# Products of the first token pair of an output projection, placed among the steps of the last attention

## The chip, the cores and the metric

The kernel runs on one core of a Trainium2 chip. The core has a matrix engine (PE in the profile, with its weight loads as PEld), a vector engine (DVE), a scalar engine (ACT), a second vector engine (POOL) and a queue processor (SP) that here issues every DMA. Each of them takes its instructions strictly in the order in which the program lists them. The metric is the time of one execution on the device in microseconds (us); lower is better.

## The reference

One decoder layer over 2048 tokens of width 1024, with 16 learned tokens put in front. Three mixers read one normalized input projection, and their gated outputs are joined to y, 2048 channels wide. What this case is about is the last of the mixers and the output projection:

```python
o_fox = fox_attention(q, k, v, log_f, valid)        # 8 heads of 64, causal
y_fox = o_fox * silu(fg)
y = concatenate([y_fox, y_gla, y_lru]) * vmask      # 2048 channels
h = h + rms_norm(y @ w_out, post_g)                 # (L,2048) @ (2048,1024)
```

## The kernel before

All of it is one unrolled program, scheduled by a framework: the Python code traces instructions in some order, a scheduler then lists them for each engine by priority (earlier traced first) and by the moment at which it thinks their inputs and buffers are ready, and it allots the buffers. `issue_after(x)` adds that an instruction may not stand before `x` on `x`'s engine. The resulting lists are fixed when the kernel is built.

**The attention.** The head pairs p = 0..3 are worked off in four chunks of 512 queries (c = 0..3). `fox_attend(k, p, c)` has 4c + 5 steps, so the last one, (3, 3), has 17, j = 0..16. A step makes the scores of 128 keys (eight matmuls into the one pair of PSUM banks `sq`), lets ACT exponentiate them into `pt` (L1305), lets DVE and POOL add `pt` to the running sums `za` (L1313), and multiplies `pt` of an earlier step with the values (`fv`, L1325). After the last step the sums go through a matmul (L1336, `fx<-za`), and the row of sums then travels: ACT copies it (L506), a DMA writes it to DRAM (L508), another brings it back spread over partitions (L510), DVE takes reciprocals (L1342, L1343), a DMA writes these (L515), two more bring them back as `rz` (L1349), POOL multiplies (L1351) and a DMA stores the attention's output into `yD` (L1352). For all chunks but the last these steps are done inside the next chunk's attention; for the last they come at its end (`end_late`).

**What runs beside it.** `merge(mix, prep, n_main, n_fill)` advances an attention and the preparation of the next job side by side; what is left of either is drained at the end. Beside the last attention runs `out_begin`, with n_fill = `OB` = 16: it loads y for the first two token blocks (t = 0, 1), loads four of the seven weight blocks (B11, T2, B21, T3) into the place where the normalized input `xhl` lay, waits nine steps, and then makes the first five parts of the halves of y (`pair_halves`).

**The output projection.** Two blocks of 128 tokens and both halves of the 1024 columns are done by a Winograd scheme with seven products in place of eight: A11·B11, S2·T2, A12·B21, S3·T3, S1·T1, A22·T4, S4·B22. Each factor is a sum of two f16 halves, so a product is 3 x 8 matmuls of 512 columns, 24 in all, on one of two PSUM banks `pj`. A pair of blocks takes 168 matmuls, and there are eight pairs (t = 0, 2, .. 14). For each pair `pair_halves` makes, on ACT, DVE and POOL: squares of y (L459), a power-of-two scale from them (DVE cast L470, a small matmul L472, DVE L316 to L320), and then for each of the seven left factors a high half on ACT (L1475) and a low half on DVE (L1476), with the sums S1 to S4 made by POOL and DVE (L1519 to L1532). `project_out` first loads the other three weight blocks (T1, T4, B22) into twelve tiles `ts`, then runs the pairs; `product` calls `next(ahead)` after each product, so that the halves are made ahead of their use: before the change five parts of a pair's halves are traced before the pair begins. `Out.finish` normalizes, adds x and stores.

All weight and y loads are 512 KB each. The lines of this document for L1475 to L1614 are those of the kernel before; the change moves them by 12 to 24 lines (L1604 becomes L1616, L1488 becomes L1512).

Of the kernel before, what the change touches and what calls it, by code (L numbers as in the profile page):

```python
# [12 lines left out]
F16 = mybir.dt.float16  # L13
I32 = mybir.dt.int32
U8 = mybir.dt.uint8
AF = mybir.ActivationFunctionType
# [5 lines left out]
P = 128  # L22
D = 1024
KT = D // P
NM = 16
SEQ = 2048
T = NM + SEQ
CH = 512
# [46 lines left out]

OB = 16
WOUT = (95, 150)
GAP = 2  # L80
FA0 = (0, 0, 1, 3, 4, 5)
# [6 lines left out]
class Ctx:  # L88
# [8 lines left out]
BUFS = {"A0": 3, "A2": 3, "KA": 6, "KB": 6, "QA": 2, "QB": 2, "B0": 2, "B1": 2, "B2": 2, "B3": 2, "V": 6, "G": 2, "R": 1,  # L97
        "T": 3, "ZZ": 8, "WR": 6, "WT": 2, "WS": 2, "TS": 12, "WC": 1, "OO": 3, "OX": 2, "LV": 5, "AT": 2, "AC": 2, "GV": 6, "GG": 6, "GS": 6, "M": 1, "MV": 1, "YG": 2, "RS": 2, "ZS": 1, "ZA": 2, "PT": 6, "ED": 2, "KT": 1, "Z": 1, "WH": 1, "WL": 1, "XC": 4, "X": 16, "L0": 4, "L1": 4, "L2": 2, "L3": 2, "L4": 6}


def unit(k, tag, shape, dt=F32, name=None):
    wide = tag in ("AT", "QA", "QB", "KA", "KB", "WC", "OO", "OX", "T", "Z", "ZZ", "WH", "WL")
    n = 1
    for d in shape[1:]:
        n *= d
    full = k.wk.tile([P, 2 * CH if wide else CH], dt, name=name or tag, tag=tag, bufs=BUFS[tag])
    ap = full[0:shape[0], 0:n]
    if len(shape) == 3:
        ap = ap.rearrange("p (a b) -> p a b", b=shape[2])
    return ap  # L110
# [39 lines left out]
def drain(g):  # L150
    for _ in g:
        pass
# [15 lines left out]
def hybrid_kernel(tc, xT, x, w_grp, w_fa, vecs, w_a2, w_r, w_i, w_out, post_g, masks, out, yD=None):  # L168
    nc = tc.nc
    with ExitStack() as es:  # L170
# [63 lines left out]
        for i, (_, _, mix, n_main, _) in enumerate(jobs):  # L234
            if i + 1 < len(jobs):
                _, prep, _, _, n_fill = jobs[i + 1]
            else:
                prep, n_fill = out_begin(k), OB
            k.todo += jobs[i][0]
# [1123 lines left out]
BLOCKS = ("B11", "T2", "B21", "T3", "T1", "T4", "B22")  # L1363
# [75 lines left out]
def wout_load(k, nm, w):  # L1439

    with k.tc.issue_after(k.mark):
        for z in range(2):
            for j in range(2):
                mark = k.nc.sync.dma_start(out=w[2 * z + j], in_=k.wD[BLOCKS.index(nm), z, j]).ins
    k.W[nm] = w
    return mark


def out_begin(k):

    nc = k.nc
    k.mark = k.dr
    k.W = {}
    n = 4 * KT // 2 * P
    views = [[k.xhl[:, (4 * i + z) * n:(4 * i + z + 1) * n].rearrange("p (q k n) -> p q k n", q=4, n=P)
              for z in range(4)] for i in range(4)]
    k.winv = k.xhl[:, 16 * n:16 * n + 2 * CH].bitcast(F32)
    raws = pair_load(k, 0)
    for i in range(4):
        k.load = wout_load(k, BLOCKS[i], views[i])  # L1460
    for q in range(4):
        nc.gpsimd.tensor_scalar(out=k.winv[:, P * q:P * q + P], in0=k.ones, scalar1=k.winvs[q], scalar2=None,
                                op0=ALU.mult)
    for _ in range(9):
        yield
    k.pairs = pair_halves(k, 0, raws)
    for _ in range(5):
        with k.tc.issue_after(k.exp):
            next(k.pairs)
        yield  # L1470


def halves(k, x, sc, hi, lo):
# [5 lines left out]
def tile4(k, tag, name):  # L1479
    return unit(k, tag, [P, KT, P], name=name)  # L1480


def y_load(k, t):
    yv = k.yD.rearrange("(h t p) n -> h p t n", p=P, h=2)
    raws = [tile4(k, "ZZ", "y") for _ in range(2)]
    for h in range(2):
        with k.tc.issue_after(k.mark):
            k.load = k.nc.sync.dma_start(out=raws[h], in_=yv[h, :, :, P * t:P * t + P]).ins  # L1488
    return raws


def y_halves(k):
    hl = k.wp.tile([P, 2, KT, P], F16, name="whl", bufs=NWB)
    return hl[:, 0], hl[:, 1]


def pair_load(k, t):
    return y_load(k, t) + y_load(k, t + 1)


def pair_halves(k, t, raws):


    nc = k.nc
    a11, a12, a21, a22 = raws
    junk = k.wk.tile([P, KT, P], BF16, name="junk", tag="A2", bufs=BUFS["A2"])
    ss = squares(k, [(x, junk) for x in (a11, a12, a21, a22)], scale=2.0)
    yield
    sc, inv = scale_of(k, ss)
    d = k.st["pair", t] = dict(inv=inv)  # L1510

    def put(nm, x):  # L1512
        d[nm] = y_halves(k)
        halves(k, x, sc, *d[nm])

    put("A11", a11)
    yield
    s1, s2 = tile4(k, "T", "s1"), tile4(k, "T", "s2")
    nc.gpsimd.tensor_tensor(s1, a21, a22, op=ALU.add)  # L1519
    nc.vector.tensor_tensor(s2, s1, a11, op=ALU.subtract)  # L1520
    put("S2", s2)
    yield
    put("A12", a12)
    yield
    nc.gpsimd.tensor_tensor(a21, a11, a21, op=ALU.subtract)
    put("S3", a21)
    yield
    put("S1", s1)
    yield
    put("A22", a22)  # L1530
    yield
    nc.gpsimd.tensor_tensor(s2, a12, s2, op=ALU.subtract)  # L1532
    put("S4", s2)


def project_out(k):
    nc = k.nc
    NT = SEQ // P
    k.mark = k.load
    for nm in BLOCKS[4:]:  # L1540
        wout_load(k, nm, [k.wk.tile([P, 4, KT // 2, P], F16, name="ts", tag="TS", bufs=BUFS["TS"])
                           for _ in range(4)])
    pg = unit(k, "WC", [P, 2, CH], name="pg")
    k.pg = [pg[:, h, :] for h in range(2)]
    with k.tc.issue_after(k.store):
        nc.sync.dma_start(out=pg.rearrange("p h n -> p (h n)"), in_=k.ins["post_g"].to_broadcast([P, 2 * CH]))
    for t in range(0, NT, 2):
        more = pair_halves(k, t + 2, pair_load(k, t + 2)) if t + 2 < NT else iter(())
        out_pair(k, t, chain(k.pairs, more))
        k.pairs = more  # L1550


class Out:
# [38 lines left out]
def out_pair(k, t, ahead):  # L1592

    nc = k.nc
    d = k.st.pop(("pair", t))
    inv = d["inv"]

    def product(nm, w):
        ps = bank(k, "pj")
        yh, yl = d.pop(nm)  # L1600
        w = k.W[w]
        for kt in range(KT):
            for j, (a, b) in enumerate(((yh, 0), (yh, 2), (yl, 0))):
                nc.tensor.matmul(out=ps, lhsT=a[:, kt, :], rhs=w[b + kt // 4][:, :, kt % 4, :], start=kt + j == 0,  # L1604
                                 stop=(kt, j) == (KT - 1, 2))
        next(ahead, None)
        return ps

    def add(ps, x, y):
        nc.vector.scalar_tensor_tensor(out=y, in0=ps, scalar=inv, in1=x, op0=ALU.mult, op1=ALU.add)  # L1610

    oa, ob = Out(k, t), Out(k, t + 1)
    c11, c12, c21, c22 = (o.o[:, n, :] for o in (oa, ob) for n in range(2))
    nc.scalar.activation(c11, product("A11", "B11"), AF.Copy, scale=inv)  # L1614
    add(product("S2", "T2"), c11, c12)
    add(product("A12", "B21"), c11, c11)  # L1616
    oa.scaled(0)
    add(product("S3", "T3"), c12, c21)
    ps = product("S1", "T1")
    add(ps, c21, c22)  # L1620
    add(ps, c12, c12)
    ob.scaled(1)
    add(product("A22", "T4"), c21, c21)
    ob.scaled(0)
    ob.finish()
    add(product("S4", "B22"), c12, c12)
    oa.scaled(1)
    oa.finish()

# [45 lines left out]
```

## Time and profile before

| | us |
|---|---|
| median of three timed runs | 1989.29 (1987.2 to 1992.66) |
| the profiled execution, its own time | 1977.47 |
| its span, first to last instruction | 1975.8 |
| PE busy in the span | 1880.4 (95%) |
| DVE, ACT, POOL busy | 1268.3, 1012.7, 565.4 |
| projection matmuls (L1604) busy: on `xhl` and on `ts` weights | 168.6 and 125.7 |

The terms below are read from the profiled execution, which was 11.8 us faster than the median of the timed ones. The page cuts the span into 40 equal slices of 49.4 us. PE is at nine tenths or more in nearly all of them; slices 32 and 33 (about 1581 to 1680 us, the end of the attention) read 8 and 7, and the clock granted to PE reads 8 in both. The DMA engines, at four tenths or less since slice 1, read 8 and 7 in slices 33 and 34.

### The profile page before, as it was taken

How to read it: one execution, taken by the hardware profiler on the slowest of the kernel's cores; microseconds unless marked ns; L12 is line 12 of the kernel's file. 1: busy time of each engine (PE TensorE's matmuls, PEld its weight loads, DVE VectorE, ACT ScalarE, POOL GpSimd, SP SyncE). 2: the span in 40 equal slices, each digit the busy share in tenths (PEclk: the TensorE clock that was granted, in tenths of full speed). 3: DMA queues.
4: the chain of work that ended last, by engine and by line, in shares of the span. 5: the costliest groups of instructions: out<-in, count | busy, mean ns of one | idle time of the engine just before them, and what ended most of it. 6: DMA issues, size and time to landing. Idle time of an engine off the chain costs nothing. (4 is left out here: it accounts for less than half of the span.)

```text
span 1975.8 us, 39430 instructions
## 1 busy us (share of the span) xinstructions
PE 1880.4 (95%) x15988; PEld 976.2 (49%) x15988; DVE 1268.3 (64%) x2850; ACT 1012.7 (51%) x1561; POOL 565.4 (29%) x548
## 2 busy tenths in 40 slices
PE   6888999999999999999999999999999987999997
PEld 5555666666555555555434443444344422444443
DVE  6766454454787788673665368747874665667674
ACT  7755642344888887762345234523442335444441
POOL 3443133221434333320122111211221124433422
PEclk9999999999999999999999999999999988999999
DMA  6200121211211100121132113412431128723411
GB/s 225 76 8 29 43 86 29 75 55 30 82 52 45 44 22 22 43 74 44 61 101 69 30 46 118 128 45 65 118 97 44 44 59 294 234 87 122 134 43 64
DMA packets 116135, 152.69 MB, mean 77 GB/s; under 512 B 18793, under 2 KB 75817, under 8 KB 115953
## 3 DMA queue, kind: packets, MB, share of 16 engines
q1 hardware_dynamic: 115952, 150.18, 24.0%
q8 instruction: 125, 2.05, 0.4%
q14 instruction: 58, 0.47, 0.1%
HBM read 108.71 MB, written 41.33 MB: 76 GB/s over the span
## 5 line engine op out<-in xcount | busy, mean ns | idle before, releaser
L485 PE MATMUL pj<-xhl,whl 128*128 128x512 f16 (+3 forms) x3960 | 813.1, 356 | 16.1 <-ACT whl L437 7.4
L485 PEld LDWEIGHTS <-whl 128*128 128x128 f16 x3984 | 364.8, 98 | 405.1 <-issue 80.7
L1305 ACT ACTIVATE pt<-sq,consts 128x1024 f32<-128x1024 f32 (+4 forms) x176 | 163.4, 929 | 252.5 <-PE sq L1303 97.7
L1313 POOL TENSOR_TENSOR za<-za,pt 128x512 f32<-128x512 f32 (+1 forms) x80 | 99.0, 1238 | 535.4 <-ACT pt L1305 489.1
L1239 DVE CUSTOM_DVE_ANT_0 mj<-mq,CB 128x512 bf16<-128x512 f32 (+4 forms) x344 | 189.9, 579 | 56.7 <-PE mq L1231 28.5
L1604 PEld LDWEIGHTS <-whl 128*128 128x128 f16 x1344 | 130.6, 98 | 160.6 <-issue 4.4
L497 PEld LDWEIGHTS <-xhl 128*128 128x128 f16 (+1 forms) x3264 | 184.9, 97 | 31.6 <-issue 27.3
L497 PE MATMUL pj<-whl,xhl 128*128 128x128 f16 (+1 forms) x3024 | 189.6, 219 | 0.0
L1313 DVE TENSOR_TENSOR za<-za,pt 128x512 f32<-128x512 f32 (+3 forms) x208 | 121.3, 606 | 84.6 <-ACT pt L1305 81.2
L1325 PE MATMUL fv<-pt,fv 128*64 128x512 f32 (+4 forms) x688 | 171.3, 538 | 0.0
L1604 PE MATMUL pj<-xhl,whl 128*128 128x512 f16 x768 | 168.6, 380 | 0.0
L1297 PE MATMUL sq<-QA,KA 64*128 64x512 f16 (+4 forms) x1032 | 127.0, 341 | 9.5 <-ACT pt L1305 9.5
L1604 PE MATMUL pj<-ts,whl 128*128 128x512 f16 x576 | 125.7, 379 | 0.0
L563 DVE SCALAR_TENSOR_TENSOR xc<-lx,consts,xc 128x448 f32<-128x448 f32 (+1 forms) x120 | 93.4, 778 | 3.6
L1588 POOL TENSOR_TENSOR o<-o,xt 128x512 f32<-128x512 f32 x31 | 51.6, 1684 | 120.3 <-issue 91.7
L1570 ACT ACTIVATE sqo<-o 128x512 bf16<-128x512 f32 x32 | 20.1, 630 | 127.7 <-DVE o L1564 127.7
L521 ACT ACTIVATE gate<-pj,consts 128x512 f32<-128x512 f32 (+2 forms) x72 | 46.1, 641 | 72.4 <-PE pj L485 59.4
L1297 PEld LDWEIGHTS <-KA 64*128 64x128 f16 (+1 forms) x1032 | 40.3, 94 | 82.5 <-issue 59.9
L1610 DVE SCALAR_TENSOR_TENSOR o<-pj,consts,o 128x512 f32<-128x512 f32 x56 | 41.1, 745 | 61.1 <-PE pj L1604 56.9
L598 POOL TENSOR_TENSOR v<-a 128x448 f32<-128x448 f32 (+1 forms) x40 | 38.4, 961 | 129.5 <-ACT a L596 115.4
L1231 PE MATMUL mq<-KA,QA 64*128 64x512 f16 (+4 forms) x344 | 60.8, 342 | 10.6 <-DVE consts L1239 9.0
L522 DVE SCALAR_TENSOR_TENSOR gate<-gate,pj 128x512 f32<-128x512 f32 (+2 forms) x72 | 45.1, 627 | 39.4 <-ACT gate L521 38.1
(263 smaller groups left out, 2786.4 us busy)
## 6 DMA issues: line engine op xcount, KB each, us to landing
wr<-in_w_out_dram SPq DMA_DIRECT2D x64, 256.0 KB
y<-yD SPq DMA_DIRECT2D x32, 512.0 KB
raw<-in_w_grp_dram SPq DMA_DIRECT2D x28, 512.0 KB
wD<-ws SPq DMA_DIRECT2D x56, 256.0 KB
CB<-c32D SPq DMA_DIRECT2D x32, 256.0 KB
rawf<-in_w_grp_dram SPq DMA_DIRECT2D x16, 512.0 KB
xhl<-wD SPq DMA_DIRECT2D x16, 512.0 KB
xt<-in_x_dram SPq DMA_DIRECT2D x16, 512.0 KB
```

Of the source, the lines that this page charges most:

```text
L485: nc.tensor.matmul(out=ps, lhsT=a[:, kt, 0:m], rhs=b[:, kt, u0:u0 + n], start=i == 0, stop=i == 23)
L497: nc.tensor.matmul(out=ps, lhsT=a[:, kt, u0:u0 + m], rhs=b[:, kt, :], start=i == 0, stop=i == 23)
L521: k.act = nc.scalar.activation(out, ps, AF.Tanh, scale=hinv).ins
L563: nc.vector.scalar_tensor_tensor(out=xc, in0=lx[:, j:j + n], scalar=cw(j), in1=xc, op0=ALU.mult, op1=ALU.add)
L1231: nc.tensor.matmul(out=ps[h][:, 0:n], lhsT=qh[hs, P * i:P * i + P], rhs=d.hi[pc][hs, 0:n], start=True, stop=pc < c)
L1239: nc.vector.tensor_tensor_reduce(out=junk[:, h, 0:n], in0=ps[h][:, 0:n], in1=d.cb[pc][:, h, 0:n], scale=1.0, scalar=-3e38, op0=ALU.add, op ...
L1297: nc.tensor.matmul(out=sp[0:m, h, off:], lhsT=a[j // 4][hs, kk], rhs=b[hs, off:], start=i == 0, stop=i == 3 and d < 0)
L1305: k.exp = nc.scalar.activation(pt[0:m, :, off:], sp[0:m, :, off:], AF.Exp, scale=K.esc[0:m]).ins
L1313: add = eng.tensor_tensor(out=za[h][0:m, off:], in0=za[h][0:m, off:], in1=pt[0:m, h, off:], op=ALU.add).ins
L1325: nc.tensor.matmul(out=pv[hs, off1:], lhsT=V1[0:m1, j1 % 4, hs], rhs=pt1[0:m1, h, off1:], start=j1 == 0, stop=j1 == nj - 1)
L1588: eng.tensor_tensor(out=o, in0=o, in1=xt[:, h, :], op=ALU.add)
L1604: nc.tensor.matmul(out=ps, lhsT=a[:, kt, :], rhs=w[b + kt // 4][:, :, kt % 4, :], start=kt + j == 0, stop=(kt, j) == (KT - 1, 2))
```

## The change

`out_begin` starts on the halves of y of the first pair at once: one idle step in place of nine, then eight steps that finish all seven factors. It then loads `post_g`, and goes on with the first pair's products themselves, by a new generator `out_next`. `product` yields after k-steps 1, 3 and 5, so that a third of a product's matmuls is one step. `OB` goes from 16 to 18: all that is past the 18th step is drained after the attention's own end. The loads of T1, T4 and B22 are traced when the tenth part of the products is reached. For the first pair `next(ahead)` is called only after three of the seven products, and the y of the second pair is loaded when the first of these calls comes; from then on two fewer parts of a pair's halves are made before the pair begins.

```diff
-OB = 16
+OB = 18
...
-    for _ in range(9):
-        yield
+    yield
     k.pairs = pair_halves(k, 0, raws)
-    for _ in range(5):
+    for _ in range(8):
         with k.tc.issue_after(k.exp):
-            next(k.pairs)
-        yield
+            next(k.pairs, None)
+        yield
+    k.mark = k.load
+    pg = unit(k, "WC", [P, 2, CH], name="pg")
+    k.pg = [pg[:, h, :] for h in range(2)]
+    with k.tc.issue_after(k.load):
+        nc.sync.dma_start(out=pg.rearrange("p h n -> p (h n)"), in_=k.ins["post_g"].to_broadcast([P, 2 * CH]))
+    k.mark = k.load
+    yield
+    for i, _ in enumerate(out_next(k, 0)):
+        if i == 9:
+            for nm in BLOCKS[4:]:
+                k.load = wout_load(k, nm, [k.wk.tile([P, 4, KT // 2, P], F16, name="ts", tag="TS", bufs=BUFS["TS"])
+                                           for _ in range(4)])
+            k.mark = k.load
+        yield
+
+
+def out_next(k, t):
+    more = iter(())
+    if t == 0:
+
+        more = (x for f in (lambda: pair_halves(k, 2, pair_load(k, 2)),) for x in f())
+    elif t + 2 < SEQ // P:
+        more = pair_halves(k, t + 2, pair_load(k, t + 2))
+    ahead, k.pairs = chain(k.pairs, more), more
+    yield from out_pair(k, t, ahead)
...
 def project_out(k):
-    nc = k.nc
-    NT = SEQ // P
-    k.mark = k.load
-    for nm in BLOCKS[4:]:
-        wout_load(k, nm, [k.wk.tile([P, 4, KT // 2, P], F16, name="ts", tag="TS", bufs=BUFS["TS"])
-                           for _ in range(4)])
-    pg = unit(k, "WC", [P, 2, CH], name="pg")
...
-    for t in range(0, NT, 2):
-        more = pair_halves(k, t + 2, pair_load(k, t + 2)) if t + 2 < NT else iter(())
-        out_pair(k, t, chain(k.pairs, more))
-        k.pairs = more
+    for t in range(2, SEQ // P, 2):
+        drain(out_next(k, t))
...
-        next(ahead, None)
+            if kt in (1, 3, 5):
+                yield
+        if t or nm in ("S1", "A22", "S4"):
+            next(ahead, None)
         return ps
...
-    nc.scalar.activation(c11, product("A11", "B11"), AF.Copy, scale=inv)
+    nc.scalar.activation(c11, (yield from product("A11", "B11")), AF.Copy, scale=inv)
```

What the scheduler makes of it, in two places. The first is SP's queue at the end of the last attention, from the last weight loads of the attention's time on; `ts<-wD` are tiles of T1, T4, B22, `y<-yD` is y of the second pair, and the rows from `rowD<-zs` to `yD<-fo` are the last attention's travel of sums. Before:

```order
L1444 DMA ts<-wD 128x2048
L1488 DMA y<-yD 128x8x128 x2
L508 DMA rowD<-zs 1x512 x2
L1488 DMA y<-yD 128x8x128 x2
L510 DMA consts<-rowD 128x8
L1444 DMA ts<-wD 128x2048 x2
L1488 DMA y<-yD 128x8x128
L515 DMA rowD<-consts 128x8
L1444 DMA ts<-wD 128x2048 x2
L1349 DMA rz<-rowD 64x512 x2
L1578 DMA xt<-in_x_dram 128x1024 x2
L1352 DMA yD<-fo 128x512
```

Now:

```order
L1444 DMA xhl<-wD 128x2048 x4
L1474 DMA pg<-in_post_g_dram 128x1024
L508 DMA rowD<-zs 1x512 x2
L510 DMA consts<-rowD 128x8
L515 DMA rowD<-consts 128x8
L1349 DMA rz<-rowD 64x512 x2
L1352 DMA yD<-fo 128x512
L1444 DMA ts<-wD 128x2048 x12
L1512 DMA y<-yD 128x8x128 x5
L1590 DMA xt<-in_x_dram 128x1024
```

All twelve `ts` loads and the y of the second pair moved from before and among the travel of sums to behind its last DMA; before, eight of the twelve `ts` loads, the eighth in the first row shown, stood ahead of the travel.

The second is ACT, from the first step of the last attention on; `pt<-sq` is a step's exponential, `junk<-y` a square, `whl` a high half. Before:

```order
L1305 ACTIVATE pt<-sq,consts 128x1024 x10
L459 ACTIVATE junk,consts<-y 128x1024 x2
L1305 ACTIVATE pt<-sq,consts 128x1024
L459 ACTIVATE junk,consts<-y 128x1024 x2
L1305 ACTIVATE pt<-sq,consts 128x1024
L1475 ACTIVATE whl<-y,consts 128x1024
L1475 ACTIVATE whl<-s_19419,consts 128x1024
L1305 ACTIVATE pt<-sq,consts 128x1024
```

Now:

```order
L1305 ACTIVATE pt<-sq,consts 128x1024
L459 ACTIVATE junk,consts<-y 128x1024 x2
L1305 ACTIVATE pt<-sq,consts 128x1024
L459 ACTIVATE junk,consts<-y 128x1024
L1305 ACTIVATE pt<-sq,consts 128x1024
L459 ACTIVATE junk,consts<-y 128x1024
L1305 ACTIVATE pt<-sq,consts 128x1024
L1499 ACTIVATE whl<-y,consts 128x1024
L1499 ACTIVATE whl<-s_19284,consts 128x1024
L1499 ACTIVATE whl<-y,consts 128x1024
L1305 ACTIVATE pt<-sq,consts 128x1024
```

The squares moved from behind the tenth exponential to behind the first, and three high halves now stand ahead of the fifth exponential (step j = 4). On PE, 60 of the first pair's matmuls now stand ahead of the attention's closing matmul L1336 (ten behind step 4's scores, two in each of the next seven steps, then 6, 6, 6, 12 and 6), where 18 stood before; behind L1336 come 36 on `xhl` weights and 72 on `ts` weights, where there were 78 and 72.

## Rows read from the trace of the kernel before

**Rows 1.** Windows view: stretch, its length; busy (count) by engine; PEclk, DMA share, GB/s.
```profile
1624.00:1676.00 52.00, 41.09 (x229) 12.11 (x225) 30.77 (x39) 28.89 (x33) 22.86 (x12) 0.89 0.87 302
1624.50:1632.10 7.60, 7.35 (x35) 1.65 (x32) 1.99 (x3) 3.94 (x4) 1.77 (x1) 0.77 1.16 314
...
1711.00:1950.00 239.00, 239.00 (x1130) 108.62 (x1129) 157.45 (x205) 99.02 (x163) 90.84 (x46) 1.00 0.33 104
...
1650.00:1660.00 10.00, 7.61 (x36) 1.96 (x34) 5.71 (x11) 8.03 (x13) 4.08 (x2) 0.84 1.02 413
```
**Rows 2.** Timeline, PE, last attention to second pair: start, length; idle before and releaser.
```profile
1640.88 0.82 PE L1297 MATMUL sq<-QA,KA 64*128 64x512 f16 x6 [0.24 <-ACT pt L1305]
...
1641.85 1.08 PE L1325 MATMUL fv<-pt,fv 128*64 128x512 f32 x4
...
1647.81 0.88 PE L1297 MATMUL sq<-QA,KA 64*128 64x512 f16 x6 [2.59 <-ACT pt L1305]
...
1649.04 1.97 PE L1325 MATMUL fv<-pt,fv 128*64 128x512 f32 x4
1650.95 1.25 PE L1297 MATMUL sq<-QA,KA 64*128 64x512 f16 x6
...
1676.06 2.18 PE L1336 MATMUL fx<-za,consts 128*64 128x512 f32 x4 [2.32 <-DVE za L1313]
1678.17 17.48 PE L1604 MATMUL pj<-xhl,whl 128*128 128x512 f16 x78
...
1711.13 20.88 PE L1604 MATMUL pj<-xhl,whl 128*128 128x512 f16 x96
```
**Rows 3.** Timeline, ACT, last attention: the fifth exponential, a square, a high half.
```profile
1633.53 1.12 ACT L1305 ACTIVATE pt<-sq,consts 128x1024 f32<-128x1024 f32 x1 [1.18 <-PE sq L1297]
...
1651.38 1.06 ACT L459 ACTIVATE junk<-y 128x1024 bf16<-128x1024 f32 x1
...
1658.75 1.15 ACT L1475 ACTIVATE whl<-y,consts 128x1024 f16<-128x1024 f32 x1 [1.91 <-issue]
```
**Rows 4.** Timeline, POOL: the first sum of a pair, for the first and second pair.
```profile
1632.12 2.35 POOL L1519 TENSOR_TENSOR s<-y 128x1024 f32<-128x1024 f32 x1 [0.21 <-DMA y<-yD]
...
1685.53 2.35 POOL L1519 TENSOR_TENSOR s<-y 128x1024 f32<-128x1024 f32 x1 [9.31 <-DMA y<-yD]
```
**Rows 5.** Timeline, DVE: a reciprocal, and steps of the first and second pair's halves.
```profile
1387.30 0.20 DVE L1342 RECIPROCAL consts<-consts 128x8 f32<-128x8 f32 x1
...
1634.50 1.23 DVE L1520 TENSOR_TENSOR s<-s,y 128x1024 f32<-128x1024 f32 x1 [3.73 <-POOL s L1519]
...
1689.05 2.32 DVE L470 CAST consts<-consts 128x4 bf16<-128x4 f32 x1
...
1696.41 0.16 DVE L316 TENSOR_SCALAR consts<-mx 128x1 int32<-128x1 int32 x1
...
1698.17 1.28 DVE L1476 SCALAR_TENSOR_TENSOR whl<-y,consts,whl 128x1024 f16<-128x1024 f32 x1 [1.03 <-ACT whl L1475]
```
**Rows 6.** Timeline, SP's DMA queue, sums of an earlier attention, few other transfers under way.
```profile
1379.32 0.66 SPq L508 DMA_DIRECT2D rowD<-zs  x2
1380.95 0.34 SPq L510 DMA_DIRECT2D consts<-rowD  x1
...
1387.85 0.33 SPq L515 DMA_DIRECT2D rowD<-consts  x1
1389.30 1.15 SPq L1349 DMA_DIRECT2D rz<-rowD  x2
...
1394.63 0.33 SPq L1352 DMA_DIRECT2D yD<-fo  x1
```
**Rows 7.** Timeline, SP's DMA queue, last attention and after it.
```profile
1636.49 0.43 SPq L1444 DMA_DIRECT2D ts<-wD  x1
...
1672.81 1.00 SPq L1488 DMA_DIRECT2D y<-yD  x2
1678.89 0.54 SPq L508 DMA_DIRECT2D rowD<-zs  x2
```

More of the change, by code (lines that the diff above doesn't have):

```diff
@@ L1463, in out_begin @@
                                 op0=ALU.mult)
-    for _ in range(9):
-        yield
-    k.pairs = pair_halves(k, 0, raws)
-    for _ in range(5):
-        with k.tc.issue_after(k.exp):
-            next(k.pairs)
-        yield
+    yield
+    k.pairs = pair_halves(k, 0, raws)
+    for _ in range(8):
+        with k.tc.issue_after(k.exp):
+            next(k.pairs, None)
+        yield
+    k.mark = k.load
[11 more added lines that the diff above has]
+            k.mark = k.load
+        yield
+def out_next(k, t):
[6 more added lines that the diff above has]
+    yield from out_pair(k, t, ahead)
 def halves(k, x, sc, hi, lo):
@@ L1536, in project_out @@
 def project_out(k):
-    nc = k.nc
-    NT = SEQ // P
-    k.mark = k.load
-    for nm in BLOCKS[4:]:
-        wout_load(k, nm, [k.wk.tile([P, 4, KT // 2, P], F16, name="ts", tag="TS", bufs=BUFS["TS"])
-                           for _ in range(4)])
-    pg = unit(k, "WC", [P, 2, CH], name="pg")
-    k.pg = [pg[:, h, :] for h in range(2)]
-    with k.tc.issue_after(k.store):
-        nc.sync.dma_start(out=pg.rearrange("p h n -> p (h n)"), in_=k.ins["post_g"].to_broadcast([P, 2 * CH]))
-    for t in range(0, NT, 2):
-        more = pair_halves(k, t + 2, pair_load(k, t + 2)) if t + 2 < NT else iter(())
-        out_pair(k, t, chain(k.pairs, more))
-        k.pairs = more
+    for t in range(2, SEQ // P, 2):
+        drain(out_next(k, t))
 class Out:
@@ L1613, in out_pair @@
     c11, c12, c21, c22 = (o.o[:, n, :] for o in (oa, ob) for n in range(2))
-    nc.scalar.activation(c11, product("A11", "B11"), AF.Copy, scale=inv)
-    add(product("S2", "T2"), c11, c12)
-    add(product("A12", "B21"), c11, c11)
+    nc.scalar.activation(c11, (yield from product("A11", "B11")), AF.Copy, scale=inv)
+    add((yield from product("S2", "T2")), c11, c12)
+    add((yield from product("A12", "B21")), c11, c11)
     oa.scaled(0)
-    add(product("S3", "T3"), c12, c21)
-    ps = product("S1", "T1")
+    add((yield from product("S3", "T3")), c12, c21)
+    ps = yield from product("S1", "T1")
     add(ps, c21, c22)
@@ L1622, in out_pair @@
     ob.scaled(1)
-    add(product("A22", "T4"), c21, c21)
+    add((yield from product("A22", "T4")), c21, c21)
     ob.scaled(0)
     ob.finish()
-    add(product("S4", "B22"), c12, c12)
+    add((yield from product("S4", "B22")), c12, c12)
     oa.scaled(1)
```

## The prediction

> **What bounds the kernel now.** I began with the page's slices: PE is full nearly everywhere, so only a stretch where PE idles can give time back, and only a new idle time of PE can cost any. The windows view shows where that is: in the 52 us of the last attention PE is busy for 41.1, so 10.9 us are idle, and the granted clock is 0.89 of full [rows 1]. Behind it, from 1711 to 1950 us, PE is busy for 239.0 of 239.0 us [rows 1]: the projection waits for nothing. The timeline of PE tells what the idle time is: short waits of 0.24 us for the exponential in nearly every step, a few waits of 2 to 2.6 us, and 2.32 us before the closing matmul L1336 [rows 2]. After a wait of 2.59 us the same four `fv` matmuls take 1.97 us, not 1.08, and the next scores 1.25, not 0.82 [rows 2]: PE ran at the lower of its two clock levels for a while, and such a fall costs at least 0.89 + 0.43 = 1.3 us. One projection matmul is worth 20.88 / 96 = 0.2175 us [rows 2].
>
> I call the start of L1336 E; it is 1676.06 us before. Then 78 + 72 = 150 matmuls of the first pair follow without a gap, and the second pair begins at 1711.13, which is E + 35.1 [rows 2]. What the change does to the whole time is what it does to that moment, since behind it PE has no gap to give or to fill.
>
> **Part 1, what is moved into the attention.** Of the first pair's 168 matmuls 60 now stand ahead of L1336, not 18: 42 x 0.2175 = 9.1 us of PE's work may fall into the 10.9 us of idle time. That is all that the change can win, if E stays where it is.
>
> **Part 2, does E stay?** The halves now stand in ACT's order ahead of the exponentials, and they depend on y. The loads of y stay where they were in the queue, so the fourth tile of y lands as before, when POOL starts its sum, at 1632.1 [rows 4]. The last of the four squares (1.06 each [rows 3]) ends at about the same time as that sum, 1634.5. From there: DVE's S2 takes 1.23 and ends at 1635.7 [rows 5], the cast and the small matmul follow by 1636.6. Then come four scale operations (0.16 each and a gap, some 0.2) and two additions of `za`, listed between them, while POOL's next subtraction (2.35, as its sum [rows 4]) holds up DVE: DVE's cast took 2.32 us beside such a subtraction [rows 5]. I put the scale at 1641; without hindrance it would be 1638.5. Three high halves of 1.15 us [rows 3] stand ahead of the exponential of step 4, so it starts at 1641 + 3.4 = 1644.4. Before, it started at 1633.53 [rows 3]: step 4 comes 10.9 us later. From there PE is the bound. Scores cost about 0.97 us a step and `fv` 1.01 (start to start [rows 2]), less in the masked steps, together 24 us for steps 4 to 16; the 60 matmuls add 13.1. Of these 37 us two are done while PE waits for the first half. So from the first low half at 1643.4 PE needs 35 us, which gives 1678.5, and one fall of the clock (PE waits some 3 us for the halves) makes it about 1680: **E moves by +4 us**. Bounds: 0, with the scale at 1638.5 and no fall; +8, where DVE, which must make seven low halves (1.28 [rows 5]) beside the `za` sums in steps 4 to 9, holds up the release of `pt`.
>
> **Part 3, the loads behind the travel of sums.** This decides. SP takes its queue in order. Before, the first `ts` load was issued at 1636.49 and the y of the second pair from 1672.81 on, ahead of the travel of sums, L508 at 1678.89 [rows 7]. Now all twelve `ts` loads and that y stand behind L1352, the last DMA of the travel, and each DMA of it waits for something. Its price, from an earlier attention with few other transfers in the queue [rows 6]: L508 to L510 1.63; L510 to the reciprocal another 1.63, an estimate by the same kind of hop; reciprocal to L515 0.55 [rows 5, 6]; L515 to L1349 1.45; L1349 to L1352 5.33; in sum 10.6. There it took 15.3 in all, since DVE was late; that is the upper bound. L508 comes 2.0 us after E (2.8 before, with the matmul at the low clock [rows 2, 7]). So the first `ts` load is issued at E + 13, with SP's own 0.4 us an issue.
>
> PE meanwhile has L1336 (1.1) and 36 matmuls on `xhl` (7.8): it is dry at E + 8.9. Twelve loads of 0.524 MB are 6.29 MB, at 413 GB/s [rows 1] 15.2 us; with 1.6 for a first landing the last one is there at E + 29.8. The first product on T1 needs three of its four tiles, E + 13 + 1.6 + 3.8 = E + 18.4: **PE waits 9.5 us**. Three products of 5.2 us, and a fall of the clock of 1.3, end the first pair at about E + 35.4.
>
> The Trainium skill ("DMA: Bandwidth & Descriptors", section Bandwidth) names about 358 GB/s as what HBM gives one core where it binds; by it the twelve loads would take 17.6 us and the sum would be 2.4 us more. The row here is at 413, so this case's trace does not agree, and I keep the row.
>
> **Part 4, y of the second pair.** Its four tiles, 2.10 MB, stand behind the `ts` loads; y moved at 314 GB/s [rows 1], 6.7 us: the last lands at E + 36.5, when PE has already ended the first pair. From there to PE's first product: from the start of POOL's sum to the end of the cast before, 1691.37 - 1685.53 = 5.8 [rows 4, 5]; the small matmul 0.3; from the first scale operation to the end of the first low half, 1699.45 - 1696.41 = 3.0 [rows 5]; and what DVE's new order puts between them, the last normalizing passes of the first pair, some 2.6. Sum 11.7: the second pair starts at **E + 48.2**, where it was E + 35.1: **+13.1 us**. Bounds: E + 44.5 if the passes and POOL's subtraction fall beside the waits; E + 52 if POOL's four final additions hold up DVE in turn. A second fall of the clock there costs 1.3.
>
> **The sum.** 4 + 13.1 + 1.3 = 18.4 us. The 9.1 us that were moved are in it: they are why PE is dry so early. Against the profiled execution, 1977.5, that is 1995.9. The median of the runs shown is 11.8 above that execution, and I add the 18.4 to the median: **1989.3 + 18.4 = 2007.7, about 2008 us**.
>
> **The rivals.**
> (a) Interleaving pays. If the loads were there when PE comes to them, 9.1 us of PE's work would be in idle time and E about where it was: 1980. The place is the T1 product; it would need T1 by E + 8.9, which is 4 us before the first load is even issued in the order above. For it: PE idles 10.9 us in that stretch [rows 1]. Against it: the order of SP's queue. The Trainium skill ("Perfetto Trace Analysis", section Optimization Strategy) says that interleaving stretches with different bounds may improve performance; by that rule this would be the outcome. No wait of the trace before bears it out behind E, as there is none. Chance 0.04.
> (b) Only the first gap shows. If the y of the second pair comes through beside the `ts` loads and its halves keep pace, the second pair starts when the first ends, E + 35.4, so +0.3, with 4 for E and 1.3 for the clock: about 1995, or 1991 if E stays. For it: the last `ts` tile lands at E + 29.8, some 5 us ahead of the first pair's end, and transfers that are in flight together may share the engines. Against: the y tiles are queued behind all twelve loads, and the 11.7 us of work behind them remain. Chance 0.1; half of it lies within 0.3% of the time before.
> (c) It costs more: the later pairs lose time too. Two fewer parts of a pair's halves are traced before it begins. In DVE's new order the scale of the next pair comes only behind the addition of the sixth product. From there: 3.0 us to the first low half [rows 5] and an addition and a scaling of at most 1.3 each, 5.6 at most, where the seventh product hides 5.2. If POOL holds DVE there by one pass, 1 to 2 us are lost in each of six pairs: +18.4 + 6 to 12, about 2017. For it: the cast that took 2.32 us [rows 5]. Against: POOL's sums for that pair come earlier in its order. Chance 0.14.
>
> **How the numbers follow.** Forecast 0.72, (a) 0.04, (b) 0.10, (c) 0.14. The forecast's own bounds are 0 + 9.4 + 0 = +9 and 8 + 16.9 + 1.3 = +26. To leave out no more than two in ten, the range reaches a little below the first, to +8, so that it leaves out (a) and most of (b), and up to +30, which takes in most of (c): 1997 to 2019. A difference of 0.3%, 6 us, is about what a measurement of this kernel can tell from none. Slower by more: forecast, (c) and half of (b), 0.9; within: 0.06; faster: 0.04.
>
> **What would show it.** PE's timeline: a gap of about 9 us in front of the first matmul on `ts` weights, released by a DMA, and a second one of some 13 us in front of the second pair, released by DVE's halves; the granted clock lower behind each. SP's timeline: the first `ts` load some 13 us after L1336. ACT's: step 4's exponential at about 1644. From the third pair on PE without gaps; gaps there would speak for (c). The forecast falls if `ts` tiles land before PE has done its 36 matmuls (a), or if the second gap is missing (b); if E is well below 1676 or above 1684, part 2 is wrong.

## The result and the profile after

The changed kernel takes 2010.15 us (median; 2006.86 to 2011.9), the kernel before beside it 1988.24 (1985.74 to 1992.66). The ratio is 1.0111, 95% interval 1.0087 to 1.0135: 21.9 us slower. The profiled execution of after took 2009.7 us, of which its span is 2008.0.

The two profiled executions are best compared from a common moment. I take **M**, the first issue of L1262 in the last attention (the DMA `QA<-dr`); up to there both programs list the same instructions, and after is already 10.0 us late there, which is no effect of the change (in the twelve profiled executions of this document M lies between 1618.5 and 1632.3). SP's queue, before:

```profile
1618.52 3.90 SPq L1262 DMA_DIRECT2D QA<-dr  x6
```

and after, there and behind the last attention:

```profile
1628.50 3.90 SPq L1262 DMA_DIRECT2D QA<-dr  x6
...
1692.55 0.53 SPq L508 DMA_DIRECT2D rowD<-zs  x2
...
1702.76 0.33 SPq L1352 DMA_DIRECT2D yD<-fo  x1
1703.25 10.07 SPq L1444 DMA_DIRECT2D ts<-wD  x12
1714.27 12.25 SPq L1512 DMA_DIRECT2D y<-yD  x5
```

Before, the first `ts` load was issued 18.0 us behind M [rows 7]; now the first of all twelve comes 74.8 us behind M, after the travel of sums. PE's timeline of after, the answer to [rows 2]:

```profile
1640.60 1.47 PE L1297 MATMUL sq<-QA,KA 64*128 64x512 f16 x6 [2.87 <-ACT pt L1305]
...
1642.42 1.97 PE L1325 MATMUL fv<-pt,fv 128*64 128x512 f32 x4
...
1649.43 0.24 PE L472 MATMUL mx<-consts 128*128 128x1 bf16 x4 [1.97 <-DVE consts L470]
...
1690.79 1.08 PE L1336 MATMUL fx<-za,consts 128*64 128x512 f32 x4
1691.80 7.94 PE L1616 MATMUL pj<-xhl,whl 128*128 128x512 f16 x36
1709.17 0.61 PE L1616 MATMUL pj<-ts,whl 128*128 128x512 f16 x1 [9.43 <-DMA ts<-wD]
1711.74 17.05 PE L1616 MATMUL pj<-ts,whl 128*128 128x512 f16 x71 [1.96 <-DMA ts<-wD]
1736.64 0.25 PE L472 MATMUL mx<-consts 128*128 128x1 bf16 x4 [7.86 <-DVE consts L470]
1738.93 2.07 PE L1616 MATMUL pj<-xhl,whl 128*128 128x512 f16 x4 [2.04 <-DVE o L1597]
1742.86 21.39 PE L1616 MATMUL pj<-xhl,whl 128*128 128x512 f16 x92 [1.86 <-DVE whl L1500]
...
1779.73 20.88 PE L1616 MATMUL pj<-xhl,whl 128*128 128x512 f16 x96
```

Read it from L1336 (E) on: 36 matmuls, a wait of 9.43 us for a `ts` tile, one matmul, another wait of 1.96 us for a `ts` tile, 71 matmuls, then 10 us without a projection matmul until the second pair's halves are there, and a slow start. From 1779.73 on, the third pair's first four products, rows are as long as before. Before, 150 matmuls stood without a gap behind L1336 [rows 2].

Two more rows show what released the second gap, POOL's first sum of the second pair (answer to [rows 4]) and what DVE and POOL did then. POOL:

```profile
1642.05 2.35 POOL L1543 TENSOR_TENSOR s<-y 128x1024 f32<-128x1024 f32 x1 [17.04 <-DMA y<-yD]
...
1730.12 2.38 POOL L1543 TENSOR_TENSOR s<-y 128x1024 f32<-128x1024 f32 x1 [27.39 <-DMA y<-yD]
1732.59 3.38 POOL L1549 TENSOR_TENSOR y<-y 128x1024 f32<-128x1024 f32 x1
1736.65 7.28 POOL L1600 TENSOR_TENSOR o<-o,xt 128x512 f32<-128x512 f32 x4 [0.68 <-DVE consts L470]
```

DVE (answer to [rows 5]):

```profile
1644.87 2.28 DVE L1544 TENSOR_TENSOR s<-s,y 128x1024 f32<-128x1024 f32 x1
...
1647.19 2.19 DVE L470 CAST consts<-consts 128x4 bf16<-128x4 f32 x1
...
1733.88 2.64 DVE L1597 SCALAR_TENSOR_TENSOR o<-o,consts,pg 128x512 f32<-128x512 f32 x1
...
1740.52 2.29 DVE L1500 SCALAR_TENSOR_TENSOR whl<-y,consts,whl 128x1024 f16<-128x1024 f32 x1
```

ACT, the first high half and the exponential of step 4 (answer to [rows 3]):

```profile
1650.81 1.15 ACT L1499 ACTIVATE whl<-y,consts 128x1024 f16<-128x1024 f32 x1 [3.44 <-DVE consts L319]
...
1653.94 1.09 ACT L1305 ACTIVATE pt<-sq,consts 128x1024 f32<-128x1024 f32 x1
```

The windows of after, the columns of [rows 1]: the stretch behind L1336, the first 5 us of the `ts` loads, the next 11, and the projection from the first pair's end.

```profile
1690.00:1720.00 30.00, 18.61 (x77) 7.36 (x76) 4.07 (x8) 1.40 (x4) 2.53 (x2) 0.83 0.58 211
...
1704.00:1709.00 5.00, 0.00 (x0) 0.00 (x0) 0.00 (x0) 0.00 (x0) 0.00 (x0) 0.57 0.98 267
1709.00:1720.00 11.00, 8.87 (x33) 3.52 (x34) 1.53 (x3) 0.00 (x0) 0.00 (x0) 0.73 1.03 415
...
1729.00:1982.00 253.00, 241.46 (x1131) 108.89 (x1131) 182.22 (x218) 106.69 (x175) 109.06 (x49) 0.97 0.36 112
```

PE is idle for 11.4 of the 30 us behind L1336, and for 11.5 of the 253 us behind the first pair.

### The profile page after: what moved, and what is told of

Its sections match the earlier page's. It is cut to its first block, busy times and chain, and to the rows that moved or that the text cites. A ratio compares the mean times of both kernels' runs of the same rounds, so it can differ in the third digit from the quotient of the medians.

```text
span 2008.0 us, 39469 instructions
## 1 busy us (share of the span) xinstructions
PE 1890.8 (94%) x15988; PEld 980.7 (49%) x15988; DVE 1280.7 (64%) x2850; ACT 1011.1 (50%) x1561; POOL 574.5 (29%) x548
## 4 chain that ended last, share of the span: by engine, by line
PE 65%; DVE 9%; ACT 5%; issue 4%; DMA 3%; POOL 3%; SPq 1%; ACTq 0%; POOLq 0%; DVEq 0%
PE pj L485 26%; PE pj L1616 13%; PE pj L497 6%; PE fv L1325 5%; PE sq L1297 5%; PE mq L1231 2%; DVE mj L1239 1%; PE st L590 1%; ACT pt L1305 1%; DVE za L1313 1%; DVE whl L438 1%; PE fx L1336 1%; POOL v L612 1%; PE mq L1235 1%; PE sq L1303 1%
## 5 line engine op out<-in xcount | busy, mean ns | idle before, releaser
L1313 POOL TENSOR_TENSOR za<-za,pt 128x512 f32<-128x512 f32 (+1 forms) x80 | 101.1, 1263 | 525.5 <-ACT pt L1305 476.5
L1313 DVE TENSOR_TENSOR za<-za,pt 128x512 f32<-128x512 f32 (+3 forms) x208 | 123.0, 614 | 85.2 <-ACT pt L1305 84.5
L1616 PE MATMUL pj<-ts,whl 128*128 128x512 f16 x576 | 128.2, 383 | 11.4 <-DMA ts<-wD 11.4
L1600 POOL TENSOR_TENSOR o<-o,xt 128x512 f32<-128x512 f32 x31 | 59.4, 1936 | 58.2 <-DVE o L1597 38.9
L1231 PE MATMUL mq<-KA,QA 64*128 64x512 f16 (+4 forms) x344 | 60.8, 342 | 11.5 <-DVE consts L1239 7.8
```

What stands on the lines that cost most here:

```text
L1231: nc.tensor.matmul(out=ps[h][:, 0:n], lhsT=qh[hs, P * i:P * i + P], rhs=d.hi[pc][hs, 0:n], start=True, stop=pc < c)
L1313: add = eng.tensor_tensor(out=za[h][0:m, off:], in0=za[h][0:m, off:], in1=pt[0:m, h, off:], op=ALU.add).ins
L1600: eng.tensor_tensor(out=o, in0=o, in1=xt[:, h, :], op=ALU.add)
```

## The experiments

Three numbers describe each kernel: E - M; S - M, where S is the start of the second pair's matmuls on PE; and the span's end less S. The last two add up to the time from M to the end, in which alone the kernels differ. They come from one profiled execution of each kernel; the ratio in the last column is that of the timed runs.

| kernel | px | E - M | S - M | end - S | from M, against before | timed ratio [95%] |
|---|---|---|---|---|---|---|
| before | 18 | 57.5 | 92.6 | 264.7 | | |
| after | 60 | 62.3 | 110.4 | 269.1 | +22.2 | 1.0111 [1.0087, 1.0135] |
| d_loads_behind | 18 | 56.5 | 104.6 | 266.7 | +14.0 | 1.0068 [1.0048, 1.0087] |
| a_ts_ahead | 60 | 61.6 | 94.2 | 268.5 | +5.4 | 1.0029 [1.0014, 1.0044] |
| b_y_ahead | 60 | 68.0 | 107.9 | 264.4 | +15.1 | 1.0071 [1.0049, 1.0092] |
| c_both_ahead | 60 | 62.4 | 86.8 | 264.7 | -5.8 | 0.9967 [0.9951, 0.9983] |
| f_fewer_products | 22 | 52.3 | 84.9 | 264.7 | -7.7 | 0.9958 [0.9939, 0.9978] |
| g_halves_later | 36 | 52.6 | 82.3 | 265.0 | -10.1 | 0.9955 [0.9934, 0.9975] |
| g_later_and_denser | 60 | 57.7 | 82.2 | 264.6 | -10.5 | 0.9964 [0.9947, 0.9980] |
| j_halves_alone | 29 | 54.8 | 85.9 | 273.5 | +2.1 | 1.0010 [0.9995, 1.0025] |
| j_halves_alone_later | 17 | 49.9 | 83.6 | 274.3 | +0.6 | 1.0006 [0.9990, 1.0022] |
| k_halves_and_lead | 26 | 53.7 | 85.5 | 264.6 | -7.1 | 0.9977 [0.9962, 0.9992] |

"px" is the number of the first pair's matmuls ahead of L1336; it is 168 less those in the rows between L1336 and S.

**d_loads_behind: the order of the loads, alone.** On the kernel before:

```diff
 def project_out(k):
-    k.mark = k.load
+    k.mark = k.store
```

> The kernel before, with one edit: the twelve loads of T1, T4, B22 and the y of the second pair stand behind the last DMA of the travel of sums (L1352); halves and products stay where they were. E is the start of L1336, and before the second pair starts at E + 35.1. Theory (the order of SP's queue costs the time): PE has 78 matmuls, 17.0 us, behind L1336 and so is dry only at E + 18.1, when the third ts tile lands (E + 18.4 in the changed kernel), so no first gap; y of the second pair lands at about E + 39 as in the changed kernel, and the second pair starts at E + 47 to E + 48, 12 to 13 us late, 1.3 to 3 us more for the clock behind the gap: ratio 1.006 to 1.008. Rival 1 (the shorter lead of the halves, two fewer parts made ahead and none before the fifth product, makes the second pair late): this kernel keeps the whole lead, so at most the first 4 us: ratio 1.000 to 1.002. Rival 2 (the delay of the attention by the halves decides): ratio 1.000.

PE's timeline, from L1336 to the second pair:

```profile
1684.74 1.63 PE L1336 MATMUL fx<-za,consts 128*64 128x512 f32 x4 [2.32 <-DVE za L1313]
1686.31 18.30 PE L1604 MATMUL pj<-xhl,whl 128*128 128x512 f16 x78
...
1730.50 0.25 PE L472 MATMUL mx<-consts 128*128 128x1 bf16 x4 [9.79 <-DVE consts L470]
1732.84 22.89 PE L1604 MATMUL pj<-xhl,whl 128*128 128x512 f16 x96 [2.10 <-ACT whl L1475]
```

No first gap to speak of (PE is busy until the `ts` tiles come), and a second one: S at E + 48.1, and 2.0 us more behind it. That is +14.0 in the trace and 1.0068 in the timed runs, as the theory had it. The lead of the halves, untouched here, is not needed to explain it, and two thirds of the change's loss come from the order of the loads without any product moved.

**a_ts_ahead, b_y_ahead, c_both_ahead: each load group put back.** On the changed kernel, a_ts_ahead:

```diff
-    for i, _ in enumerate(out_next(k, 0)):
-        if i == 9:
-            for nm in BLOCKS[4:]:
-                k.load = wout_load(k, nm, [...])
-            k.mark = k.load
+    for nm in BLOCKS[4:]:
+        k.load = wout_load(k, nm, [...])
+    k.mark = k.load
+    for _ in out_next(k, 0):
```

b_y_ahead; c_both_ahead has both edits:

```diff
+    k.raws2 = pair_load(k, 2)
     for i, _ in enumerate(out_next(k, 0)):
...
-        more = (x for f in (lambda: pair_halves(k, 2, pair_load(k, 2)),) for x in f())
+        more = pair_halves(k, 2, k.raws2)
```

> The changed kernel with the twelve ts loads traced right behind the load of post_g, so that they stand ahead of the last travel of sums; y of the second pair stays behind it. Theory: no wait of 9.4 us in front of the first matmul on ts weights; the first pair ends at E + 25; y of the second pair is issued at about E + 12, lands at E + 21, and the second pair starts 8.8 us later, at E + 30 (before E + 35.1, changed kernel E + 48.1). With E later by 4.75 and 4.4 lost behind the start of the second pair as in the changed kernel: 4.75 - 5 + 4.4 = +4 us on the kernel before, ratio 1.002 (1.000 to 1.004). Rival 1 (shorter lead): the halves of the second pair are called for only at the fifth product, which now comes earlier, so it gives the same start and does not differ here. Rival 2 (the weight loads were not the cause of the first gap): the gap stays, ratio 1.009 or more.

The first gap is gone, the second is shorter, since y is issued at E + 13.8, not E + 23.5. PE and POOL (two fences):

```profile
1695.98 15.27 PE L1615 MATMUL pj<-ts,whl 128*128 128x512 f16 x70
1717.75 0.25 PE L472 MATMUL mx<-consts 128*128 128x1 bf16 x4 [6.50 <-DVE consts L470]
```

```profile
1711.88 2.34 POOL L1542 TENSOR_TENSOR s<-y 128x1024 f32<-128x1024 f32 x1 [11.36 <-DMA y<-yD]
```

y landed at E + 24.7 where E + 21 was expected, so S is at E + 32.6, not E + 30; the whole is in the expected interval.

> The changed kernel with y of the second pair loaded before the first product is traced, so that its loads stand far ahead of the last travel of sums; the ts loads stay behind it. Theory: the wait of about 9 us in front of the first ts matmul stays, the first pair ends at E + 37 to 38, and the second pair starts there at once, not 10 us later: 4.75 + 2.9 + 1.3 = +9 us on the kernel before, ratio 1.0045 (1.003 to 1.006). Rival 1 (the shorter lead of the halves makes the second pair late, whenever y lands): a gap of 5 to 10 us in front of the second pair stays, released by DVE's low half; ratio 1.008 to 1.011.

The second gap is gone, as expected, and nothing is lost behind S; but the whole is 6 us above the expectation, because E is 5.7 us later than in after. POOL, ACT and PE:

```profile
1674.01 2.34 POOL L1544 TENSOR_TENSOR s<-y 128x1024 f32<-128x1024 f32 x1 [1.68 <-DMA y<-yD]
```

```profile
1677.60 1.11 ACT L1305 ACTIVATE pt<-sq,consts 128x1024 f32<-128x1024 f32 x1 [4.20 <-POOL za L1313]
```

```profile
1678.77 0.68 PE L1297 MATMUL sq<-QA,KA 64*128 64x400 f16 x6 [3.62 <-ACT pt L1305]
...
1712.84 0.61 PE L1617 MATMUL pj<-ts,whl 128*128 128x512 f16 x1 [6.76 <-DMA ts<-wD]
```

With the load, its consumer moved forward too: POOL's sum of the second pair's y now stood among the `za` sums of the last steps, waited for its tile, and held an exponential for 4.2 us. The first gap stayed (3.0 + 6.8 us around the small matmul).

> The changed kernel with both edits: the ts loads and y of the second pair stand ahead of the last travel of sums. Theory: neither gap; PE runs from L1336 into the second pair at E + 25 (before E + 35.1): 4.75 - 10.1 = -5.4, and 1.3 to 4.4 lost to the clock behind: -4 to -1 us on the kernel before, ratio 0.998 to 0.9995. Rival 1 (shorter lead of the halves): a gap of 5 us or more in front of the second pair, ratio 1.001 to 1.004. Rival 3 (loads crowd the last attention, E later than 62 us behind the landing of QA): E later by 3 us or more, ratio 1.001 or more.

```profile
1691.30 1.08 PE L1336 MATMUL fx<-za,consts 128*64 128x512 f32 x4
1692.31 7.94 PE L1616 MATMUL pj<-xhl,whl 128*128 128x512 f16 x36
1700.09 10.52 PE L1616 MATMUL pj<-ts,whl 128*128 128x512 f16 x48
...
1715.73 20.88 PE L1616 MATMUL pj<-xhl,whl 128*128 128x512 f16 x96
```

Neither gap, S at E + 24.4, and nothing lost behind it: -5.8 us in the trace, 0.9967 timed. The 1.3 to 4.4 us that the expectation set aside for the clock did not arise, so the ratio lies below its range. E is as late as in after, so all of 22.2 + 5.8 = 28 us between the two kernels is the place of these sixteen loads. Nothing is lost behind S although the lead of the halves is the shorter one of the change: the shorter lead is not to blame.

**f_fewer_products, g_halves_later, g_later_and_denser: the moved matmuls and the place of the halves.** All on c_both_ahead. f_fewer_products sets `OB = 12`; g_halves_later has four idle steps ahead of the halves; g_later_and_denser has five, and `OB = 22`:

```diff
-    yield
+    for _ in range(4):
+        yield
     k.pairs = pair_halves(k, 0, raws)
```

> The kernel of the run c_both_ahead (both load groups ahead of the travel) with 12 in place of 18 steps of the first pair's work beside the attention: the halves keep their place in the first steps, but 22 of the first pair's matmuls stand ahead of L1336, not 60. M is the first issue of L1262 in the last attention; E, the start of L1336, was M + 57.5 before and M + 62.4 in c_both_ahead, the second pair started at M + 92.6 and M + 86.8. Theory P (once the halves are there PE is full, and the moved matmuls push E by their own length): E = M + 62.4 - 38 x 0.2175 = M + 54.1 to M + 56; 146 matmuls behind it, the second pair starts at M + 86.8 to M + 88.9, and the whole differs from c_both_ahead by 2 us at most: ratio 0.997 to 0.998. Rival Q (the moved matmuls lie in idle time of PE, and the wait for the halves alone holds E at M + 60 to 62.4): the second pair starts at M + 93 to M + 95, ratio 1.000 to 1.001.

E came at M + 52.3 and S at M + 84.9. So theory P holds, and more: with 38 matmuls fewer ahead of E, E is 10.1 us earlier, where their own length is 8.3. Moving them forward had not won anything. (The timed ratio lies below the expected range; its interval overlaps with that of c_both_ahead.) Where the win over the kernel before comes from shows in the windows of the two halves of the stretch from M to E. Before:

```profile
1618.50:1644.50 26.00, 20.03 (x100) 5.32 (x98) 9.13 (x16) 9.51 (x9) 6.08 (x4) 0.82 0.74 229
1644.50:1676.00 31.50, 23.67 (x136) 7.11 (x132) 22.42 (x26) 19.96 (x25) 16.78 (x9) 0.89 0.83 312
```

c_both_ahead:

```profile
1628.90:1654.30 25.40, 15.05 (x58) 3.58 (x54) 11.30 (x18) 12.28 (x16) 7.31 (x3) 0.74 0.76 242
1654.30:1691.30 37.00, 36.42 (x220) 11.74 (x218) 23.76 (x26) 18.12 (x20) 17.39 (x10) 1.00 0.81 306
```

f_fewer_products:

```profile
1627.00:1652.00 25.00, 15.30 (x64) 3.60 (x62) 9.89 (x18) 12.20 (x17) 8.23 (x4) 0.66 0.83 273
1652.00:1679.30 27.30, 27.24 (x178) 7.99 (x174) 25.17 (x25) 16.70 (x18) 14.78 (x9) 1.00 0.83 288
```

Before, PE was idle for 7.8 of the last 31.5 us, at a clock of 0.89, while the halves were made there. With the halves early it is idle for 0.1 to 0.6 us, at full clock. The price stands in the first half: 9.7 to 10.4 us idle, at 0.66 to 0.74, where 6.0 were idle before.

> The kernel of the run c_both_ahead with four idle steps in place of one: the first high halves stand ahead of the exponential of step 6, not 4, and 36 of the first pair's matmuls stand ahead of L1336, not 60. M and E as in f_fewer_products. Theory (E is late because the exponential of step 4 waits for the scale of y, which is there at M + 22.4 to 23): steps 4 and 5 run on while y lands and is summed, and the exponential of step 6 (M + 21.2 before) comes at M + 25 to 26; 24 matmuls fewer ahead of E take 5.2 us off: E = M + 56 to M + 58.5, the second pair starts 29.8 us behind E at M + 86 to M + 88; ratio 0.9965 to 0.998, so what E gains the thinner filling gives back. Rival (the place of the halves does not matter, E follows the clock and the loads): E stays at M + 60 to 62, the second pair at M + 90 or later, ratio 0.999 or more.

> The kernel of the run c_both_ahead with five idle steps in place of one and 22 in place of 18 steps: two high halves stand ahead of the exponential of step 6 (as in g_halves_later), and 62 of the first pair's matmuls ahead of L1336, most of them in the last, masked steps. M and E as in f_fewer_products. Theory (both help: no wait for the scale in steps 4 and 5, and the matmuls fill the later steps): E = M + 58 to M + 61, the second pair starts 24.4 us behind E at M + 82.5 to M + 85.5: 7 to 10 us faster than the kernel before, ratio 0.995 to 0.9965. Rival (from the halves on PE is full in c_both_ahead already, and steps 4 and 5 only move the same wait to step 6): E = M + 62, the second pair at M + 86 to 87 as in c_both_ahead, ratio 0.997.

Both reach S at M + 82, 4 us earlier than expected for the first and just below the range of the second: about 10 us faster than the kernel before in the trace, 0.9955 and 0.9964 timed (intervals that overlap with c_both_ahead and with each other). With two steps more ahead of the halves the first stretch loses less (in g_halves_later PE is idle for 7.4 of its 25.7 us, at a clock of 0.80); and 36 or 60 matmuls ahead of E give the same S. What is ahead of E delays E by its length, as in f_fewer_products.

**j_halves_alone, j_halves_alone_later, k_halves_and_lead: the halves without products.** On the kernel before (j_halves_alone_later has four idle steps):

```diff
-    for _ in range(9):
+    for _ in range(1):
         yield
     k.pairs = pair_halves(k, 0, raws)
-    for _ in range(5):
+    for _ in range(8):
         with k.tc.issue_after(k.exp):
-            next(k.pairs)
+            next(k.pairs, None)
```

> The kernel before with one part of the change alone: one idle step in place of nine and all halves of the first pair in the next eight; no products, loads or leads are touched. Two high halves stand ahead of the exponential of step 4, 29 of the first pair's matmuls ahead of L1336 (18 before). M is the first issue of L1262 in the last attention. Theory after f_fewer_products (E was early there although the halves stood early: before, the halves in the last steps held up the exponentials and sums, and that idle time of PE goes once they are early): E = M + 52 to M + 54 (before M + 57.5), 139 matmuls behind it, the second pair starts at M + 83.5 to M + 86: 6.5 to 9 us faster, ratio 0.9955 to 0.9967. Rival (the early halves cost the attention 4.75 us, as the changed kernel's E suggests, and f_fewer_products gained by its loads): E = M + 60 to 62, second pair at M + 91 to 93, ratio 0.999 to 1.0005.

> As j_halves_alone, but with four idle steps: two high halves ahead of the exponential of step 7 instead of step 4, 17 of the first pair's matmuls ahead of L1336. If the wait for the scale of y in front of step 4 costs E anything beside what PE does later, E is 1 to 2 us earlier than in j_halves_alone; if PE's own work or the sums decide, the same. Second pair at M + 85 to M + 87 by its 12 matmuls more behind E, ratio 0.9962 to 0.9972.

In j_halves_alone S came as the theory had it (M + 85.9) and E 0.8 us behind its range; with the later start of the halves E came 4.9 us earlier still, not 1 to 2, but 2.6 of these are the twelve matmuls fewer ahead of it, and S is 2.3 us earlier. But neither kernel is faster: 9 to 10 us are given back behind S, which no expectation had foreseen. PE, ACT, DVE and POOL of j_halves_alone (four fences):

```profile
1714.80 10.52 PE L1604 MATMUL pj<-xhl,whl 128*128 128x512 f16 x48
1731.44 0.27 PE L472 MATMUL mx<-consts 128*128 128x1 bf16 x4 [6.12 <-DVE consts L470]
```

```profile
1725.21 1.15 ACT L1475 ACTIVATE whl<-s,consts 128x1024 f16<-128x1024 f32 x1 [1.28 <-POOL o L1588]
1726.27 1.04 ACT L459 ACTIVATE junk<-y 128x1024 bf16<-128x1024 f32 x1
```

```profile
1729.10 2.28 DVE L470 CAST consts<-consts 128x4 bf16<-128x4 f32 x1 [1.16 <-ACT junk L459]
```

```profile
1715.49 2.65 POOL L1519 TENSOR_TENSOR s<-y 128x1024 f32<-128x1024 f32 x1 [6.26 <-DMA y<-yD]
```

The small matmul of the third pair's scale stands only 48 matmuls into the second pair. DVE's cast ahead of it waits for the third pair's squares, and these stand in ACT's order behind the first pair's normalizing and a high half. (The next expectation puts this wait to the landing of y; but y was there when POOL's sum began, at 1715.49, and these rows say that it was the order on ACT.) The suspect is the lead: with all halves of the first pair made early, each `next(ahead)` within the first pair runs two parts further into the next pairs (the next expectation says three): seven parts of the second pair's halves, not five, are traced before it begins, and the small matmul stands behind 48 matmuls, not 96. k_halves_and_lead takes that back:

```diff
-        next(ahead, None)
+        if t or nm in ("S1", "A22", "S4"):
+            next(ahead, None)
```

> j_halves_alone with one more part of the change: for the first pair the next pair's halves are called for only after the products on S1, A22 and S4. In j_halves_alone the second pair started at M + 85.9, 6.7 us earlier than before, but PE lost 8.8 us inside it: the small matmul of the third pair's scale stood behind its 48th matmul and waited 6.12 us for the third pair's y. Theory (all parts of the first pair's halves are made early, so each call in the first pair now runs the next pairs' halves three parts further ahead, past the landing of y; the later call takes that back): the small matmul stands behind 144 matmuls, no wait in the second pair, E and the start of the second pair as in j_halves_alone (M + 54 to 56, M + 85 to 87), the whole 5.5 to 7.5 us faster than before: ratio 0.996 to 0.9972. Rival (the third pair's y or its sums are late whatever the lead, since its loads stand behind the travel): a wait of 4 us or more moves to the end of the second pair, ratio 0.999 to 1.001.

```profile
1716.06 20.88 PE L1604 MATMUL pj<-xhl,whl 128*128 128x512 f16 x96
```

The second pair runs through, and end - S is back at 264.6: 7.1 us faster in the trace. The timed ratio, 0.9977 [0.9962, 0.9992], lies a little above the expected 0.996 to 0.9972; its interval reaches into it. So the later `next(ahead)` of the change is the part that it needs, not the one that hurts.

## Why the prediction was right

It said 2008 us and slower; it was 2010.15. By its own steps, each against M:

- **Part 1** (60 matmuls ahead of L1336, 36 behind on `xhl`): as read from the order.
- **Part 2, E +4**: E - M went from 57.5 to 62.3, +4.75. The exponential of step 4 came at M + 25.4 (the prediction's 1644.4 is M + 25.9), held by a scale whose S2 and cast each took 2.2 to 2.3 us. The granted clock was 0.60 from 1628.5 to 1653.9 (`fv` 1.97 at 1642.42) and 1.00 from there to L1336, where the prediction counted one short fall.
- **Part 3, the first gap**: L1352 at E + 12.0, the first `ts` load at E + 12.5, PE dry at E + 8.95, first matmul on `ts` at E + 18.4, wait 9.43; predicted 12.6, 13, 8.9, 18.4 and 9.5. That the last two agree is luck. The prediction let the product start with the landing of its third tile; here one matmul ran on the first tile, and the next, which needs the third (`product` takes the tiles from 0 and from 2 in turn), waited 1.96 us more, to E + 20.95. So the first pair's end was mis-sized: E + 38.0, not 35.4. The rate of 413 GB/s from [rows 1] was not at fault. The `ts` loads moved 415 from 1709 to 1720, but only 267 in the 5 us before; why they start slowly stays open. The figure that the prediction quotes from the Trainium skill ("DMA: Bandwidth & Descriptors", section Bandwidth), about 358 GB/s, lies between the two; these rows do not show it as a limit.
- **Part 4, the second gap**: S at E + 48.1 against E + 48.2, but this too is luck. The prediction counted to the end of the first low half; S is earlier, since PE's first four matmuls take high halves alone. The first low half ended at E + 52.0 (L1500, 1740.52 + 2.29), the prediction's upper bound: y landed at E + 39.3, not 36.5, and from POOL's sum to that low half it took 12.7 us, not 11.7. As that bound had it, POOL's four final additions (L1600, from 1736.65) ran beside DVE, and the low half took 2.29, not 1.28. Less the four matmuls that were done by then, the second pair is 16.1 us late, not 13.1. This is the term of the sum that was most mis-sized.
- **The term behind it**, 1.3 us for the clock, is about right: the 92 matmuls behind the low half took 21.39 and not 20.0. That end - S grew by 4.4 is this, the wait of 1.86 for the first low half, and the four matmuls in 2.07 and not 0.87, at a granted clock of 0.50. With 4.75 for E and 16.1 for the second gap the sum is 22.2, where the prediction had 18.4.
- **The base**: the profiled execution of after stands 32.2 us above that of before, of which 10.0 arose before M. To add the sum to the median and not to the profiled time was right: 18.4 against 21.9 in the timed runs.

What was wrong in the reasons: "That is all that the change can win", 9.1 us of moved matmuls. f_fewer_products shows that the moved matmuls win nothing; k_halves_and_lead, where no product and no load is traced elsewhere than before, shows that the early halves win what there is, 7.1 us in the trace, by leaving the last steps of the attention. Rival (a) would have needed the loads ahead of the travel, and c_both_ahead, where they are, wins 5.8 of the 9.1 us that it promised, and by another cause. Rival (b) failed on the queue as argued. Rival (c), that a shorter lead costs the later pairs, is refuted by c_both_ahead and turned round by j_halves_alone, where the longer lead cost 9 us.

Three things stay open: why the first `ts` loads are slow, why E in f_fewer_products came 1.8 us earlier than its matmuls explain (one high half, not three, stands there ahead of the exponential of step 4), and which of g_halves_later and g_later_and_denser is faster.

## What to carry to other kernels

When a change traces loads later, look first where they land in the issuing queue: loads that need nothing, behind DMAs that wait for results, cost here 28 us, more than the whole rest of the change was worth. Matmuls moved into a stretch in which PE is already full only move its end; what pays is to take other engines' work out of the stretch where PE waits for them. And work that is made earlier lengthens every lead that is counted in steps behind it: check where the next stage's small, waiting instructions now stand in each in-order queue.

## What the runs showed of the hardware

- The `ts` loads alone moved 415 GB/s from 1709 to 1720, with a DMA share of 1.03; a mix with `xhl` loads had moved 413 at 1.02 [rows 1]. In their first 5 us the share was 0.98 as well, but they moved 267.
- DVE's passes with two inputs took about twice as long or more beside POOL: S2 2.28 at 1644.87, beside L1313 and L1549 (1.23 before), a low half 2.29 at 1740.52 beside L1600 (1.28), L1597 2.64 beside L1549 (0.74 at the least). The Trainium skill ("SBUF — State Buffer", section Who interferes with whom) says that a DVE instruction with two SBUF inputs contends with a GpSimd instruction that reads SBUF; the trace agrees.
- In the first steps of the last attention PE waits 2 to 3 us now and then (2.87 at 1640.60, 1.97 at 1649.43). In after the granted clock of the stretch from 1628.5 to 1653.9 was 0.60, and the `fv` at 1642.42 took 1.97 us, not 1.08, at the lower of PE's two levels (1.2 of 2.4 GHz). In c_both_ahead and f_fewer_products that stretch has a clock of 0.74 and 0.66, in g_halves_later 0.80; before, it had 0.82. This is a price of halves that are made early.
